# Collecting the sample columns of the feature-major projections in one SBUF tile before they go to DRAM

## The chip, the cores and the metric

The kernel runs on one core of one Trainium2 chip. The metric is the device time of one execution in microseconds (us); the median of three runs is quoted. Instructions run on TensorE (PE, with its weight loads as PEld), VectorE (DVE), ScalarE (ACT), GpSimd (POOL) and SyncE (SP). SP does no arithmetic here: it issues most DMAs, in order, from one queue; ACT issues some from its own.

## The reference

One inference step of a two-layer decoder, for a prompt of 2048 tokens and for a sample group of 8 rows with one token each; both share the weights. In each layer:

```
hn   = rms_norm(x) * norm_w
proj = hn @ w_in[l]                       # 1024 -> 3336 columns, split into 15 pieces
r_q, r_k, r_v, r_g                        # retention, rotary on q and k
m_q, m_k, m_v, m_o, m_g, m_i, m_f         # mLSTM
s_u, s_g                                  # S5, a diagonal complex state space model
a_q, a_g                                  # attention into 256 memory tokens
mix  = [ret | mlstm | s5 | memxattn], each times silu of its gate
y    = x + mix @ w_out[l]
```

A last RMSNorm follows. The sample rows go through the same projection, then start from states and caches that are inputs. All results are float32.

## The kernel before

**Tiling.** The prompt is cut into four units of 512 tokens (b = 0 to 3) per layer (l = 0, 1). A unit runs the groups of `ORDER`, each 256 columns of `w_in` (or of `w_out` for out0 to out3 of the unit before it). Matrices are split into a high and a low float32r part, so a product costs three matmuls per 128 rows of contraction. From b = 1 on the split weights come back from DRAM (`ws`), in 8 loads of 256 KB per group.

**Two layouts.** Groups in `FEAT` (m_k, m_q, a_q, s_g, a_g, s_u, r_q) are computed feature-major by `feat_bank`: PSUM holds 128 features by up to 512 tokens, in two halves m. The others are token-major.

**The sample columns.** The 8 sample rows ride along in unit b = 1 of each layer as columns 512 to 519 of `hT`. There a feature-major half is computed in two pieces of 260 columns, and the last 8 columns of the second piece are the sample's. `group` copies them with VectorE into a small tile of 128 x 8 (`sm`, line 480) and stores that with a DMA into `sproj[l]`, a DRAM tile of 8 rows by 3336 columns. The address pattern is

```python
self.dma(AP(self.sproj[l], COL[g] + 128 * m, [[1, 128], [D_IN, NB]]), o)
```

so each of the 1024 elements goes to a place of its own: neighbours in a partition lie 3336 floats apart, and the partitions lie 4 bytes apart. There are 7 groups x 2 halves x 2 layers = 28 such stores. For token-major groups `sample_group` stores whole rows of 256 columns from a tile of 8 partitions (`sproj<-so`).

**Who reads them.** After group r_g of unit b = 1, `sample_layer` starts as a side generator. It reloads every piece from `sproj` in the layout that it wants (`sq`, `sqs`, `srv`, `smq` and so on). Later `sample_s5` fills `uT`, the s_u columns with features on partitions 96 to 127, with 8 DMAs of 32 x 8 single elements.

**Order.** `build` steps the main generator and then all side generators (S5, mLSTM, retention and attention of the prompt, and the sample's). The instruction order on each engine and each DMA queue is then settled by the tile framework, which runs its own timeline when it schedules; it may move independent instructions past each other. S5 of the prompt (`s_core`) stores U to DRAM (`ud<-U`), reads it back permuted on ACT's queue (`X<-ud`, line 194), and loads tables per quarter on SP's (`sTW`, `sWi`, `sCS`); its matmuls are `ps<-X,sWi` and `ps<-X,sTW`. Its result goes through DRAM too, by eight DMAs `yd<-Y` per unit, in pieces of 128 floats. The mLSTM of the prompt makes `E`, `RT`, `rows` and `sm` (lines 799 to 943).

Line 181 is the matmul helper `mm`, line 185 the transpose helper `tr`, line 188 the ACT helper `act`, lines 191 and 194 the DMA helpers of SP and of ACT.

Of the kernel before, what the change touches and what calls it, by code (L numbers as in the profile page):

```python
# [28 lines left out]
D_IN = 3336  # L29
# [4 lines left out]
NB = 8  # L34
WB = 16
KEPT = (0, 1, 2, 3)
FEAT = ("m_k", "m_q", "a_q", "s_g", "a_g", "s_u", "r_q")

COL = dict(r_q=0, r_k=256, r_v=512, r_g=768, m_q=1024, m_k=1280, m_v=1536, m_o=1792, m_g=2048,
           m_if=2304, s_u=2312, s_g=2568, a_q=2824, a_g=3080)  # L40
# [74 lines left out]
def AP(t, off, ap):  # L115
    return bass.AP(tensor=t.tensor, offset=t.offset + off, ap=[list(x) for x in ap])


class Builder:
# [93 lines left out]
    def setup(self):  # L213
        nc, I, cp = self.nc, self.I, self.cp
        c = lambda n, s, dt=F32: cp.tile(s, dt, name=n, tag=n)
        self.ident = c("ident", [128, 128])
        self.dma(self.ident, I["c_ident"])
        self.wstream()
        self.mem_load()
        self.wload(0)  # L220
        self.hnl = self.hn_load(0, 0)
        next(self.hnl)
        self.wload(1)
        self.maskb = c("maskb", [128, 512], BF16)
        self.identb = c("identb", [128, 128], BF16)
        mt = self.t2([128, 512])
        self.dma(mt, I["c_mask"])
        nc.vector.tensor_copy(self.maskb, mt)
        nc.vector.tensor_copy(self.identb, self.ident)
        self.Dt = c("Dt", [128, 2, 2, 128])  # L230
        self.dma(self.Dt, I["c_D"])
        self.vd = c("vd", [128, H])
        self.dma(self.vd, I["c_vd"])
        self.ropes = c("ropes", [128, 2, 16])
        self.dma(self.ropes, I["c_ropes"])
        self.smc = c("smc", [128, 4])
        self.dma(self.smc, I["c_sm"])
        self.e127 = c("e127", [128, 1])
        self.dma(self.e127, I["c_e127"])
        self.s32 = c("s32", [128, 32])  # L240
        self.dma(self.s32, I["c_s32"])
        self.s8 = c("s8", [128, 8])
        self.dma(self.s8, I["c_s8"])
        st = self.t2([128, H])
        self.dma(st, I["c_sel"])
        self.sel = c("sel", [128, H], F32R)
        nc.vector.tensor_copy(self.sel, st)
        zero = self.t2([128, 320])
        nc.vector.memset(zero, 0.0)
        self.ones = c("ones", [128, 1])  # L250
        nc.vector.memset(self.ones, 1.0)

        self.hT = [cp.tile([128, 8, UT + NB], F32R, name=f"hT{i}", tag=f"hT{i}") for i in range(2)]
        self.Sr = [c(f"Sr{i}", [128, 2, 128]) for i in range(3)]
        self.Cm = [c(f"Cm{i}", [128, 2, 130]) for i in range(3)]
        for t in self.Sr + self.Cm:
            nc.vector.memset(t, 0.0)
        self.mprev = c("mprev", [4, 8])
        self.hS = [c(f"hS{i}", [128, 8, 40], F32R) for i in range(2)]
        for i in range(2):  # L260
            nc.vector.tensor_copy(self.hS[i].rearrange("p a b -> p (a b)"), zero)

        T = self.T
        self.xd = [self.dram([T, D], f"xd{i}") for i in range(self.depth)]
        self.xsd = [self.dram([NB, D], f"xsd{i}") for i in range(self.depth)]
        self.sproj = [self.dram([NB, D_IN], f"sproj{i}") for i in range(self.depth)]
        self.smix = [self.dram([NB, D], f"smix{i}") for i in range(self.depth)]
        self.stab = []
        self.memd = []
        for l in range(self.depth):  # L270
            self.stab.append(dict(
                Wi=self.dram([128, SG, 128], f"Wi{l}"), TW=self.dram([128, 3, 1024], f"TW{l}"),
                CS=self.dram([128, 2, SG, 128], f"CS{l}"), Kd=self.dram([32, 16, 112], f"Kd{l}"), ab=self.dram([128, 3, SG], f"ab{l}"),
                C1=self.dram([128, SG, SC], f"C1{l}")))
            self.memd.append((self.dram([128, 2, MEM], f"mk{l}"), self.dram([128, 2, GW], f"mv{l}")))
# [173 lines left out]
    def group(self, i):  # L449
        kind, l, b, g = self.wseq[i]  # L450
        if i == 0:
            self.wsplit(0, 0)
            self.wsplit(0, 1)
        hi, lo, _ = self.wspl[i]
        if kind == "mem":
            self.mem_group(l, b, hi, lo)
            self.advance(i, 0)
            self.advance(i, 1)
            yield
        elif kind == "out":  # L460
            if self.sample_in_unit(kind, l, b):
                while not self.smix_done[l]:
                    self.step_sides()
                self.sample_group(i, l, g, hi, lo, kind)
            yield from self.group_out(i, l, b, g, hi, lo)
        elif g in FEAT:
            if g == "r_q":
                for m in range(2):
                    self.u["rq", m] = self.g4([128, 2, UT], n="rqt")
                    self.dmaa(self.u["rq", m], self.I["c_rq"][b, m])  # L470
            smp = self.sample_in_unit(kind, l, b)
            pieces = [(0, 260), (260, 520)] if smp else [(0, UT)]
            for m in range(2):
                for c0, c1 in pieces:
                    ps = self.feat_bank(m, hi, lo, slice(c0, c1))
                    c2 = min(c1, UT)
                    self.evac_f(l, b, g, m, ps[:, :c2 - c0], slice(c0, c2))
                    if c1 > UT:
                        o = self.sm([128, 16])[:, :NB]
                        self.nc.vector.tensor_copy(o, ps[:, c2 - c0:c1 - c0])  # L480
                        self.dma(AP(self.sproj[l], COL[g] + 128 * m, [[1, 128], [D_IN, NB]]), o)
                    if (c0, m) == (0, 0):
                        self.advance(i, 0)
                    if c1 >= UT and m == 1:
                        self.advance(i, 1)
                    yield
        else:
            if g == "m_v":
                jobs = [[t] for t in range(4)]
            else:  # L490
                jobs = [[0, 1], [2, 3]]
            n = 264 if g == "m_v" else 256
            for m, ts in enumerate(jobs):
                sls = [slice(t * 128, (t + 1) * 128) for t in ts]
                ps = self.tok_bank(sls, n, hi, lo, self.hslice)
                self.evac(l, b, g, m, ps)
                if m in (0, len(jobs) - 1):
                    self.advance(i, min(m, 1))
                if g == "r_g":
                    nxt = self.next_unit(l, b)  # L500
                    if nxt:
                        self.hn_T(2 * m)
                        self.hn_T(2 * m + 1)
                yield
        if kind == "in" and g not in FEAT and self.sample_in_unit(kind, l, b):
            self.sample_group(i, l, g, hi, lo, kind)
# [1031 lines left out]
    def sample_group(self, i, l, g, hi, lo, kind):  # L1538
# [16 lines left out]
        else:  # L1555
# [5 lines left out]
            if g == 3:  # L1561
# [3 lines left out]
                else:  # L1565
                    w = self.bcrow(self.I["final_norm_w"])
                    self.rms_rows([self.xrow], w[:NB], NB)
                    self.dma(self.O["y_sample"].rearrange("b o d -> (b o) d"), self.xrow)

    def s_load(self, t, l, name, width, off=0, outer=True):  # L1570


        for q in range(4):
            o = COL[name] + (q * 16 if width == 16 else 0)
            self.dma(t[32 * q:32 * q + 32], AP(self.sproj[l], o, [[D_IN, NB], [DH, H], [1, width]]))
# [197 lines left out]
    def sample_s5(self, l, lc):  # L1773
        nc, v, gp, I, O = self.nc, self.nc.vector, self.nc.gpsimd, self.I, self.O
        tab, dr = self.stab[l], self.sproj[l]
# [6 lines left out]

        uT = self.s64([128, 8, NB], n="suT")
        for pr in range(8):
            self.dma(uT[96:128, pr, :], AP(dr, COL["s_u"] + 32 * pr, [[1, 32], [D_IN, NB]]))
        st = self.t1([128, 2, 128], n="sst")
        for w, nme in enumerate(("state_s5_re", "state_s5_im")):
            src = I[nme][l].rearrange("b g p -> (b g) p")
# [3 lines left out]
        ps = self.bank()  # L1792
# [18 lines left out]
        ps = self.bank()  # L1811
# [17 lines left out]
        ps = self.bank()  # L1829
# [15 lines left out]
        g, th = self.t1([128, GW], n="sgg")[:NB], self.t1([128, GW], n="sgh")[:NB]  # L1845
# [144 lines left out]
```

## Time and profile before

| | |
|---|---|
| median of 3 runs | 2325.03 us (2319.82 to 2328.7) |
| the profiled execution, its own time | 2328.93 us |
| its span, first to last instruction | 2327.1 us |
| PE busy | 2160.1 us, 93% |
| DVE, ACT, POOL busy | 61%, 33%, 17% |
| mean granted TensorE clock | 0.962 of full speed |
| DMA packets | 392905, of which 115800 under 512 B |

The span is the time from the first to the last instruction; the execution's own time is 1.8 us more. The mean granted clock is 1 at 2.4 GHz and 0.5 at 1.2 GHz. A matmul record can last longer because the clock is low, so a busy PE is not always a PE at its peak.

### The profile page before, as it was taken

Reading aid. Unit: us, or ns where it says so; the run is one execution under the profiler, and the core shown is the slowest. Engines: PE = TensorE matmul, PEld = TensorE weight load, DVE = VectorE, ACT = ScalarE, POOL = GpSimd, SP = SyncE. Lnnn points to the kernel's source line nnn. Section 1 sums busy time; section 2 is a strip of 40 time slices with the busy share of each in tenths; the row PEclk is TensorE's granted clock in tenths of the full one; section 3 lists DMA queues with packets and bytes.
Section 4 is the critical chain, followed back from the end, with each engine's and each line's share of the span. In section 5 each row is a group of like instructions: output and inputs, shape, how many; then the busy total and the mean of one; then the engine's idle time right before and its main releaser. Section 6 shows DMA issues by size and latency. Waiting matters only on the chain. (4 is left out here: it accounts for less than half of the span.)

```text
span 2327.1 us, 44458 instructions
## 1 busy us (share of the span) xinstructions
PE 2160.1 (93%) x16386; PEld 1991.0 (86%) x16386; DVE 1424.2 (61%) x3883; ACT 778.3 (33%) x1842; POOL 405.5 (17%) x435
## 2 busy tenths in 40 slices
PE   7889977899999999989899999898999899999998
PEld 6688967899997888888798989887899788888888
DVE  7787855535465687565944768355465466656463
ACT  4445422323223332134422454222331233312332
POOL 3343111111001113120202331110100001121011
PEclk9999988999999999989999999898999999999999
DMA  7878587978686656877568884996877776598634
GB/s 223 297 251 270 201 163 140 225 257 139 175 276 202 219 187 214 294 146 230 160 199 281 267 275 149 242 287 132 176 142 258 273 222 209 185 315 211 180 116 153
DMA packets 392905, 496.88 MB, mean 214 GB/s; under 512 B 115800, under 2 KB 216344, under 8 KB 392688
## 3 DMA queue, kind: packets, MB, share of 16 engines
q1 hardware_dynamic: 366848, 433.61, 64.3%
q10 hardware_dynamic: 25840, 60.43, 8.8%
q8 instruction: 129, 2.11, 0.4%
q14 instruction: 88, 0.72, 0.1%
HBM read 376.75 MB, written 118.21 MB: 213 GB/s over the span
## 5 line engine op out<-in xcount | busy, mean ns | idle before, releaser
L181 PE MATMUL pm<-hT,w 128*128 128x512 f32 (+1 forms) x3360 | 681.4, 358 | 9.2 <-ACT w L188 5.9
L181 PEld LDWEIGHTS pm<-hT,w 128*128 128x128 f32 x3360 | 550.7, 193 | 98.1 <-ACT w L188 6.5
L181 PE MATMUL pm<-w,hT 128*128 128x256 f32 (+1 forms) x4608 | 607.8, 288 | 12.8 <-DMA w<-ws 5.0
L181 PEld LDWEIGHTS pm<-w,hT 128*128 128x128 f32 x4608 | 574.1, 193 | 21.4 <-DMA w<-ws 7.2
L181 PE MATMUL pm<-w,mix 128*128 128x256 f32 x3072 | 379.8, 285 | 3.7 <-ACT w L188 2.1
L181 PEld LDWEIGHTS pm<-w,mix 128*128 128x128 f32 x3072 | 372.8, 192 | 4.9 <-ACT w L188 2.3
L366 POOL TENSOR_TENSOR w<-w,w 128x512 fp32r<-128x512 f32 (+1 forms) x76 | 110.0, 1448 | 370.4 <-ACT w L188 158.9
L188 ACT ACTIVATE w<-w 128x512 fp32r<-128x512 f32 (+1 forms) x152 | 95.0, 633 | 181.2 <-DMA w<-w_in 78.1
L1358 POOL TENSOR_TENSOR sA<-sy,sCS 128x512 f32<-128x512 f32 x32 | 53.0, 1658 | 363.1 <-DVE sy L1355 162.0
L366 DVE TENSOR_TENSOR w<-w,w 128x512 fp32r<-128x512 f32 (+1 forms) x76 | 54.6, 720 | 87.7 <-ACT w L188 73.2
L188 ACT ACTIVATE Pt<-ps,sm 128x256 f32<-128x256 f32 x128 | 58.9, 472 | 114.5 <-DVE sm L994 93.0
L1454 DVE TENSOR_TENSOR xr<-xr,pm 128x512 f32<-128x512 f32 x56 | 38.2, 684 | 78.2 <-PE pm L181 32.4
L188 ACT ACTIVATE sB<-ps 64x512 f32<-64x512 f32 x64 | 37.9, 592 | 107.9 <-DVE sy L1347 83.7
L1355 DVE TENSOR_TENSOR_SCAN sy<-ab,xprev,sy 128x128 f32<-128x128 f32 x128 | 57.3, 505 | 0.6
L1414 POOL TENSOR_TENSOR t<-t,s_g 128x512 f32<-128x512 f32 x16 | 25.4, 1584 | 175.2 <-DVE t L1412 83.7
L643 POOL TENSOR_TENSOR r_k<-rp 128x256 f32<-128x256 f32 x32 | 24.2, 759 | 181.8 <-DVE rp L641 160.3
L993 DVE TENSOR_REDUCE sm<-ps 128x2 f32<-128x512 f32 x64 | 42.3, 685 | 21.2 <-PE ps L181 20.9
L181 PE MATMUL ps<-X,sWi 128*128 128x128 f32 x256 | 38.6, 297 | 17.2 <-DMA sWi<-Wi 11.2
L588 POOL TENSOR_TENSOR r_qT<-rqs,rqs 128x512 f32<-128x512 f32 (+2 forms) x20 | 22.0, 1100 | 184.5 <-DVE rqs L587 100.3
L898 POOL TENSOR_TENSOR vw<-mv,RT 128x260 f32<-128x260 f32 x32 | 22.1, 699 | 178.5 <-DVE sm L1109 69.4
L181 PEld LDWEIGHTS ps<-X,sWi 128*128 128x128 f32 x256 | 33.1, 202 | 21.6 <-issue 21.5
L185 PE MATMUL ps<-ident,xt 128*128 128x128 f32 x256 | 38.2, 300 | 13.2 <-DVE xt L387 11.5
(434 smaller groups left out, 3308.5 us busy)
## 6 DMA issues: line engine op xcount, KB each, us to landing
w<-ws SPq DMA_DIRECT2D x768, 256.0 KB
ws<-w SPq DMA_DIRECT2D x256, 256.0 KB
w<-w_in SPq DMA_DIRECT2D x104, 256.0 KB
sCS<-CS SPq DMA_DIRECT2D x32, 512.0 KB
xd<-xr SPq DMA_DIRECT2D x56, 256.0 KB
w<-ws SPq DMA_DIRECT2D x48, 264.0 KB
sTW<-TW SPq DMA_DIRECT2D x32, 384.0 KB
xt<-x_prompt ACTq DMA_DIRECT2D x16, 512.0 KB
```

Of the source, the lines that this page charges most:

```text
L181: self.nc.tensor.matmul(out, lhsT, rhs, start=start, stop=stop, skip_group_check=skip)
L185: self.nc.tensor.transpose(out, in_, self.ident[:K, :K])
L188: self.nc.scalar.activation(out, in_, f, **kw)
L366: e.tensor_tensor(lo[q], r[q], hi[q].bitcast(F32), OP.subtract)
L588: self.nc.gpsimd.tensor_tensor(u["r_qT"][:, m, c], q, qs, OP.add)
L643: gp.tensor_tensor(dst[:, x, :], t1.rearrange("p h f -> p (h f)"), t2.rearrange("p h w f -> p (h w f)"), OP.add)
L898: gp.tensor_tensor(vw, mv[:, j], RT[:, j, 3, :, None].to_broadcast([128, H, 65]), OP.mult)
L993: v.tensor_reduce(mx[:, 2 * x:2 * x + 2], ps[x].rearrange("p (a m) -> p a m", a=2), AX.X, OP.max)
L1355: v.tensor_tensor_scan(t1[:, g], self.abt[:, 2, gg:gg + 1].to_broadcast([128, 128]), t1[:, g], self.xprev[:, gg:gg + 1], OP.mult, OP.add)
L1358: gp.tensor_tensor(A[:, :, 1:129], t1, Cs, OP.mult)
L1414: gp.tensor_tensor(zg.rearrange("p (j s) -> p j s", s=4), z.rearrange("p (s j) -> p j s", s=4), u["s_g", m].rearrange("p (j s) -> p j s", ...
L1454: v.tensor_tensor(xr, xr, ps.rearrange("p (t c) -> p t c", t=2), OP.add)
```

## The change

The sample columns of all 14 feature-major halves of a layer are copied into one tile `sft` of 128 x 14 x 8, one slot per half. When the fourteenth is in, a new side generator `sample_feat` transposes the tile once on TensorE (112 rows of 128), copies the result to SBUF with ACT, and stores it with seven DMAs, one per group, each 16 rows of 128 contiguous floats. `sample_s5` fills `uT` with eight ACT copies out of `sft` in place of eight DMAs from `sproj`.

```diff
                     if c1 > UT:
-                        o = self.sm([128, 16])[:, :NB]
-                        self.nc.vector.tensor_copy(o, ps[:, c2 - c0:c1 - c0])
-                        self.dma(AP(self.sproj[l], COL[g] + 128 * m, [[1, 128], [D_IN, NB]]), o)
+                        if "sft" not in self.u:
+                            self.u["sft"] = self.tb([128, 2 * len(FEAT), NB], "sft")
+                            self.u["sft_n"] = 0
+                        self.nc.vector.tensor_copy(self.u["sft"][:, 2 * FEAT.index(g) + m, :], ps[:, c2 - c0:c1 - c0])
+                        self.u["sft_n"] += 1
+                        if self.u["sft_n"] == 2 * len(FEAT):
+                            self.sides.append(self.sample_feat(l, self.u["sft"]))
...
+    def sample_feat(self, l, sft):
+
+        self.sft[l] = sft
+        yield
+        n = 2 * len(FEAT) * NB
+        ps = self.bank()
+        self.tr(ps[:n, :128], sft.rearrange("p g b -> p (g b)"))
+        o = self.t1([128, 264], n="sfo")
+        self.act(o[:n, :128], ps[:n, :128])
+        for i, g in enumerate(FEAT):
+            self.dma(AP(self.sproj[l], COL[g], [[128, 2], [D_IN, NB], [1, 128]]), o[2 * NB * i:2 * NB * (i + 1), :128])
...
         for pr in range(8):
-            self.dma(uT[96:128, pr, :], AP(dr, COL["s_u"] + 32 * pr, [[1, 32], [D_IN, NB]]))
+            self.act(uT[96:128, pr, :], self.sft[l][32 * (pr % 4):32 * (pr % 4) + 32, 2 * FEAT.index("s_u") + pr // 4, :])
```

## Rows read from the trace of the kernel before

**Rows 1.** The page: span, and busy time, share and instructions of PE.

```profile
span 2327.1 us, 44458 instructions
PE 2160.1 (93%) x16386; PEld 1991.0 (86%) x16386; DVE 1424.2 (61%) x3883; ACT 778.3 (33%) x1842; POOL 405.5 (17%) x435
```

**Rows 2.** Windows by unit: length, busy time of each engine, clock, DMA share, GB/s.

```profile
267.10:607.10 340.00, 298.10 (x2448) 286.27 (x2447) 181.63 (x453) 106.77 (x271) 48.20 (x46) 0.92 0.78 177
607.10:862.90 255.80, 248.90 (x1850) 226.97 (x1849) 159.21 (x519) 79.77 (x190) 26.89 (x36) 0.99 0.70 219
862.90:1141.40 278.50, 267.33 (x1960) 240.04 (x1958) 189.18 (x470) 89.37 (x208) 60.23 (x74) 0.97 0.70 211
1141.40:1422.90 281.50, 267.16 (x1974) 243.93 (x1975) 176.22 (x437) 108.73 (x245) 58.98 (x54) 0.97 0.74 239
1422.90:1730.60 307.70, 276.79 (x2310) 267.93 (x2308) 164.31 (x445) 97.89 (x247) 39.63 (x41) 0.93 0.82 192
1730.60:1984.40 253.80, 247.06 (x1846) 225.48 (x1845) 146.52 (x442) 74.80 (x185) 21.09 (x23) 0.99 0.71 234
1984.40:2257.20 272.80, 264.12 (x1939) 237.98 (x1938) 168.61 (x430) 77.08 (x197) 43.30 (x34) 0.98 0.68 202
```

**Rows 3.** Tile sproj: the DMAs, ns min/median/max to issue, first and last start.

```profile
L191 SPq DMA_DIRECT2D sproj<-sm x28: 367/385/1882, 306.7 to 1713.8; - x28
...
L191 SPq DMA_DIRECT2D suT<-sproj x16: 302/432/884, 940.5 to 2069.6; - x16
```

**Rows 4.** Windows before and after the first store, and while yd is stored.

```profile
295.00:306.00 11.00, 11.00 (x101) 10.43 (x100) 10.55 (x33) 4.03 (x11) 5.27 (x5) 1.00 0.86 289
309.00:314.00 5.00, 5.00 (x44) 5.00 (x44) 3.20 (x12) 1.29 (x4) 0.00 (x0) 1.00 1.00 81
1871.00:1875.00 4.00, 4.00 (x19) 3.26 (x18) 3.23 (x13) 0.08 (x1) 0.00 (x0) 1.00 1.00 338
```

**Rows 5.** DMA rate in 40 slices of 1 us, from 360 us on.

```profile
GB/s 16 45 137 279 379 294 320 54 25 23 10 48 31 71 66 180 250 397 385 412 373 262 303 147 8 3 36 32 41 47 41 269 179 0 16 0 0 0 0 0
```

**Rows 6.** Timeline of SP: a store in that stretch; four stores of yd.

```profile
361.63 0.43 SPq L191 DMA_DIRECT2D sproj<-sm  x1
...
1871.11 1.83 SPq L191 DMA_DIRECT2D yd<-Y  x4
```

**Rows 7.** Timeline of SP, ACT, DVE and PE, 320 to 335 us.

```profile
321.85 0.82 SPq L191 DMA_DIRECT2D sproj<-sm  x1
...
330.60 2.63 ACTq L194 DMA_DIRECT2D X<-ud  x4
333.28 0.66 ACT L188 ACTIVATE mkT<-pm 128x260 f32<-128x260 f32 x2 [11.14 <-issue]
333.97 0.17 DVE L480 COPY sm<-pm 128x8 f32<-128x8 f32 x1 [11.18 <-ACT mkT L188]
334.36 0.58 PE L181 MATMUL ps<-sm,e 128*128 128x16 f32 x2 [7.38 <-DVE sm L862]
```

**Rows 8.** Windows, PE alone, low-clock stretches of each b = 1 unit, with sums.

```profile
332.20:349.30 17.10, 8.98 (x40) 0.50 0.80 124
...
sum 54.80, PE 36.59; mean PE 5.23
...
sum 41.00, PE 27.90; mean PE 5.58
```

**Rows 9.** Tile and group views: what the new transpose and copies are like.

```profile
L185 PE MATMUL ps<-ident,mkT x64: 270/272/421, 104.0 to 2090.5; 128*128 128x128 f32 x64
...
L188 ACT ACTIVATE sso<-ps 128x128 f32<-128x128 f32 x2 | 0.6, 278 | 17.9 <-PE ps L185 14.9 <-issue 3.0
```

**Rows 10.** Timeline of SP: the first sample load of layer 1.

```profile
1729.15 0.76 SPq L191 DMA_DIRECT2D sq<-sproj  x1
```

**Rows 11.** Waits of SP's queue.

```profile
SPq L191 <- PE pm L181: 325.6, 233, 18.6
...
SPq L191 <- DVE sm L480: 15.9, 6, 8.7
```

More of the change, by code (lines that the diff above doesn't have):

```diff
@@ L268, in setup @@
         self.stab = []
+        self.sft = {}
         self.memd = []
```

## Prediction

> **What bounds the kernel now.** I read the page first. PE is busy for 2160.1 of 2327.1 us, so time comes back only where PE stands still or runs at its low clock [rows 1]. The next view is the windows, cut where each unit's last r_g bank is evacuated. The reader should compare the two b = 1 units, rows one and five of the table, with the other five [rows 2]. They last 340.0 and 307.7 us; the others 253.8 to 281.5. They are the units that carry the sample columns. They have more PE work, but PE is also idle in them for 340.00 - 298.10 = 41.9 and 307.70 - 276.79 = 30.9 us, against 6.9, 11.2, 14.3, 6.7 and 8.7 in the others, on average 9.6. The granted clock is 0.92 and 0.93 against 0.97 to 0.99. And their DMA engines are the busier ones for less work: shares of 0.78 and 0.82 at 177 and 192 GB/s, where the others have 0.68 to 0.74 at 202 to 239.
>
> The view of the tile sproj shows what is special there: 28 stores `sproj<-sm`, the first at 306.7 us, the last at 1713.8 [rows 3]. SP needs 0.385 us to issue one, so the issue is cheap. The windows around the first one show the price. Before it the DMA engines move 289 GB/s at a share of 0.86; from 309 to 314 us they move 81 GB/s at a share of 1.00 [rows 4]. They are full and deliver little. In slices of 1 us from 360 us on the rate is 279 to 379 GB/s in the four slices from 363 to 367, then eight slices in a row stay under 75, and from 384 seven more do [rows 5]. The first of these runs follows the store issued at 361.63 us, once the packets ahead of it are through [rows 6]. So one store of 4 KB blocks the engines for some 8 us, and everything in their queues waits with it.
>
> How that reaches PE is seen in the timeline from 320 to 335 us [rows 7]. The store of 321.85 us goes out while ACT wants to issue `X<-ud`; it reads back what `ud<-U` has stored, and starts only at 330.60. ACT's queue is in order, so the evacuation of mkT waits behind it, 11.14 us in all. The copy at line 480 reads the same bank and waits 11.18 us on VectorE's queue, and a small PE matmul behind that finds PE idle for 7.38 us. After such a gap the clock falls to the lower of the two levels, 0.50 from 332.2 to 349.3 us; summed over such stretches PE is busy at half clock for 36.59 us in the first of the units and for 27.90 us in the second [rows 8].
>
> **The change, part by part.** *Removed: 28 scattered stores.* All of the excess is an upper bound. Idle time is 41.9 + 30.9 = 72.8 us [rows 2]. Work done at half clock takes twice as long, so half of 36.59 + 27.90, or 32.2 us, is lost to the clock [rows 8]. Together 105.0 us. Not all of it will go, since units without these stores have idle time too. I let the two units sink to the level of the other five: 9.6 us idle each, and a clock loss that I scale. There the mean clock misses 2% of 268.5 us, or 5.4 us [rows 2]; in the b = 1 units the loss of 32.2 us stands against a missing 0.08 x 340.0 + 0.07 x 307.7 = 48.7 us of clock, a share of 0.66, as part of the low clock falls on idle time. So 0.66 x 5.4 = 3.6 us stay. What stays is 2 x (9.6 + 3.6) = 26.4 us, and the gain is 105.0 - 26.4 = 78.6 us. The lower bound is that only the waits nearest to the stores go and other waits appear behind them. I put it at half of that, 39 us. I take 78.6 because the mechanism repeats at each store and because nothing else sets these units apart from their neighbours.
>
> A second working gives the same order. The b = 1 units moved about 340.0 x 177 = 60 MB and 307.7 x 192 = 59 MB; their neighbours 255.8 x 219 = 56 and 253.8 x 234 = 59 MB [rows 2]. The load on the queues is not larger, so without the blocks these loads can flow as in a neighbour.
>
> *Replaced: where the copy goes.* The 28 copies stay as they are, 128 x 8, 0.17 us [rows 7]. No gain and no loss.
>
> *Added: transpose, copy, seven stores per layer.* One transpose of 128 x 112 takes about 0.27 us, as the row of mkT has it, so 0.5 us of PE in all [rows 9]. One ACT copy of 112 x 128 takes about 0.28 us, as `sso` does [rows 9]; ACT is busy for 106.77 and 97.89 us of these units and has room [rows 2]. Seven issues replace fourteen on SP, at about 0.385 us each [rows 3], so SP gains 2.7 us per layer, which hides behind its other waits. The stores write 16 pieces of 512 B each. How such pieces fare is visible in `yd<-Y`: four DMAs are issued from 1871.1 us on, and the engines move 338 GB/s at a share of 1.00 [rows 4, 6]; these are pieces of 512 B too, by their address pattern. So I take the seven at nothing on the engines; the bound is one old store's block, 8 us of engine time per layer, spread over PE as before: 78.6 / 28 = 2.8 us each, 5.6 us for two.
>
> *Moved: when the rows reach DRAM.* All feature-major groups now arrive after the last half of a_g. In layer 1 the last store goes out at 1713.8 us [rows 3], and the first reload `sq<-sproj` is issued at 1729.15 us [rows 10]. That leaves 15.4 us for a transpose, a copy and 7 x 0.385 = 2.7 us of issues. If the cover were gone, SP would hold at `sq` with the weight loads behind it, for at most the missing time.
>
> *Removed: 16 loads of uT; added: 16 ACT copies.* SP loses eight issues of 0.43 us per layer [rows 3]. A copy of 32 x 8 is bounded by 0.28 us, so ACT gets 2.2 us per layer [rows 9], in units where it is busy for 77 to 89 of 270 us [rows 2]. The loads read single elements and start at 940.5 us [rows 3], in units with the ordinary idle time; I count no gain.
>
> Sum: 2328.93 - 78.6 + 0.5 = 2250.8 us for an execution like the profiled one. That execution lies 3.9 us above the median of the runs, so for the median 2246.9, or 2247 us.
>
> **The rivals.** *Half of it (the partial case).* The stalls go, but the waits move to other loads of the same queues, because PE's order is dense and ACT and SP still hold at every DMA that waits. The gain is 39 us, the time 2286. For it: the SP queue waits 325.6 us for PE in any case [rows 11], and the units' order was made with these stores in it. Against it: neighbours with as many bytes show 9.6 us of idle time.
>
> *The stores were never the cost.* If a 4-byte piece costs only its own slot, 1024 pieces are 64 on each of 16 engines, and the low rate has another source, such as the `yd` and `ud` traffic of S5, which stays. Then PE's gaps stay, and with the added 0.5 us the time is 2325.5 us. For it: 4 KB is next to nothing beside the 60 MB of a unit. Against it: yd's own stores leave the rate at 338 GB/s, with no such fall as from 309 to 314 us [rows 4], and the other five units have the same S5 traffic without the idle time.
>
> The Trainium skill, page "DMA: Bandwidth & Descriptors", section "Why small descriptors are slow (HBM only)", gives a fixed overhead of some 3 bus cycles per piece and 32 B of metadata; with the 850 MHz that it names for the fabric, my estimate from it is 64 x 4 cycles, 0.3 us per store. By that rule the removed stores were worth 28 x 0.3 = 8 us of hidden DMA time, this rival holds and the time would be about 2325; the 5 us at a share of 1.00 and 81 GB/s differ from it, and I go by the row.
>
> *Slower.* The seven stores stand in SP's in-order queue and wait for the ACT copy, which waits for the transpose, which waits in PE's order for the last copy of a_g. Weight loads behind them wait too. The old stores did this for VectorE's copy six times, 8.7 us at the longest; SP's longest wait of all is 18.6 us [rows 11]. To eat the gain and 12 us more, the hold would have to cost PE (78.6 + 12) / 2 = 45 us per layer. At the longest wait shown, twice 18.6, the result is 2247 + 37 = 2284, still faster; beyond 45 us per hold, some 2337.
>
> *More than all.* Loads run ahead so well that nothing of the excess stays: 105 us and some knock-on, 2215.
>
> **How the numbers follow.** What a measurement can tell from no change is about 0.5%, 11.6 us. I draw the line between the forecast and the partial case midway, at a gain of 59 us. Chances: my forecast, 59 to 105 us, 0.66; the partial case, 12 to 59 us, 0.22; no change 0.06; slower 0.03; more than all 0.03. So faster has 0.91, no change 0.06, slower 0.03. The range runs from 2218 (the upper bound, 105 us, and 2 more) to 2288 (just past the partial case). What it leaves out is the last three cases, 0.12, and some 0.06 of the partial one.
>
> **What the new profile would show.** Right: no `sproj<-sm`; 14 stores of rows, after a_g; b = 1 units of about 340.0 - 47 = 293 and 307.7 - 32 = 276 us, with idle time near 10 us and a clock of 0.97 or more; no run of slices under 75 GB/s at a full share. The unit figures are the excess of each: 41.9 + 18.3 - 13.2 = 47 less what the new work takes, and 30.9 + 14.0 - 13.2 = 32. Wrong: low rates at full share remain, then the stores were not the cause; or the rate is high and PE still waits, then the order or the queues hold it. A long SP wait ahead of the seven stores would be the slower case.

## The result, and the profile after

The changed kernel takes 2223.44 us, median of 4 runs (2219.64 to 2227.03), against 2326.75 us for the kernel before, beside it: a ratio of 0.956 with an interval of 0.953 to 0.959. That is 103 us less. The forecast was 2247 us within 2218 to 2288. The direction was right; the gain was 78.6 us on paper and is larger by 25.

The page of the changed kernel: PE does the same work in a shorter span, and the small packets are fewer by 33000, the 28672 elements of the stores and the 4096 of the uT loads among them.

```profile
span 2223.7 us, 44414 instructions
...
PE 2128.1 (96%) x16388; PEld 1965.0 (88%) x16388; DVE 1426.7 (64%) x3883; ACT 782.1 (35%) x1860; POOL 404.9 (18%) x435
...
DMA packets 359685, 496.86 MB, mean 223 GB/s; under 512 B 82356, under 2 KB 183124, under 8 KB 359468
```

The windows by unit of the changed kernel, columns as in [rows 2]. The first and the fifth are the b = 1 units.

```profile
265.90:554.70 288.80, 282.79 (x2449) 273.33 (x2448) 181.41 (x455) 107.60 (x271) 47.16 (x46) 0.99 0.65 209
554.70:813.20 258.50, 249.38 (x1849) 227.10 (x1848) 158.98 (x519) 79.81 (x189) 27.01 (x36) 0.98 0.68 217
813.20:1083.80 270.60, 264.34 (x1960) 237.79 (x1958) 189.70 (x469) 91.14 (x216) 60.37 (x75) 0.99 0.71 217
1083.80:1367.10 283.30, 268.60 (x1974) 245.43 (x1975) 177.42 (x438) 108.80 (x246) 59.08 (x53) 0.96 0.73 237
1367.10:1629.80 262.70, 262.70 (x2309) 256.37 (x2308) 165.09 (x444) 97.68 (x247) 39.95 (x41) 1.00 0.66 226
1629.80:1884.40 254.60, 248.23 (x1847) 226.66 (x1845) 146.58 (x442) 74.80 (x184) 21.08 (x23) 0.99 0.71 232
1884.40:2154.40 270.00, 262.04 (x1939) 236.22 (x1938) 171.08 (x430) 78.61 (x205) 43.34 (x34) 0.99 0.69 205
```

Beside [rows 2]: the b = 1 units fall from 340.0 to 288.8 and from 307.7 to 262.7 us, together by 96.2 of the 103.4 us of span. Their idle time falls from 41.9 to 6.0 and from 30.9 to 0.0 us, their clock rises to 0.99 and 1.00, and the DMA engines are less busy (0.65 and 0.66) while they move more in the same time (209 and 226 GB/s). Of the other five, the two b = 3 units (third and last row) are shorter by 7.9 and 2.8 us; the rest are longer, by up to 2.7 us.

The low-clock stretches of the first of these units, PE alone, answer to [rows 8]: 6.8 us in place of 54.8. In the second there are none.

```profile
326.70:330.10 3.40, 3.40 (x16) 0.50 0.64 191
391.50:394.90 3.40, 3.40 (x17) 0.50 1.05 366
```

The DMA rate in 40 slices of 1 us from 300 us on, while s_u and m_k are computed, answers to [rows 5]: one slice alone is under 98 GB/s.

```profile
GB/s 266 326 365 406 310 109 217 285 242 269 310 307 213 207 215 307 387 397 369 365 261 214 182 235 261 282 98 109 164 340 82 301 252 301 289 387 402 402 385 154
```

What the new work costs, from the views of the tiles sft and sfo (ns min/median/max, first and last start):

```profile
L483 DVE COPY sft<-pm x28: 134/160/168, 305.0 to 1611.0; 128x8 f32<-128x8 f32 x28
L188 ACT ACTIVATE suT<-sft x16: 204/206/208, 886.9 to 1949.4; 32x8 f32<-32x8 f32 x16
...
L185 PE MATMUL ps<-ident,sft x2: 270/270/270, 537.3 to 1612.8; 128*112 128x128 f32 x2
...
L191 SPq DMA_DIRECT2D sproj<-sfo x14: 567/567/707, 537.9 to 1617.2; - x14
L188 ACT ACTIVATE sfo<-ps x2: 277/278/279, 537.6 to 1613.1; 112x128 f32<-112x128 f32 x2
```

SP's timeline from the stores of rows to the first reload, in layer 0 and then in layer 1:

```profile
537.88 4.46 SPq L191 DMA_DIRECT2D sproj<-sfo  x7
...
554.20 0.75 SPq L191 DMA_DIRECT2D sq<-sproj  x1
```

```profile
1613.37 4.44 SPq L191 DMA_DIRECT2D sproj<-sfo  x7
1617.91 3.73 SPq L191 DMA_DIRECT2D w<-ws  x8
1621.74 0.49 SPq L191 DMA_DIRECT2D sproj<-so  x1
1622.28 0.72 SPq L191 DMA_DIRECT2D sq<-sproj  x1
```

The DMA engines while the seven stores of layer 0 go out, and right after, in windows with the columns of [rows 4]:

```profile
539.00:543.00 4.00, 4.00 (x36) 3.96 (x36) 3.99 (x5) 0.98 (x2) 0.00 (x0) 1.00 0.05 14
544.00:546.00 2.00, 2.00 (x20) 2.00 (x19) 0.00 (x0) 0.00 (x0) 0.00 (x0) 1.00 0.97 314
```

And the waits of SP's queue, as in [rows 11]:

```profile
SPq L191 <- ACT sfo L188: 16.1, 2, 9.7
```

The transpose and the copy cost what [rows 9] said. An issue of the row stores takes 0.567 us, not 0.385, and the seven take 4.46 us with the gaps between them. They leave the engines at a share of 0.05. SP does hold for the ACT copy, up to 9.7 us, in layer 1. PE pays nothing for it: the unit in which that hold lies has no idle time at all.

### The profile page after: what moved, and what is told of

It reads as the page before. It is cut to its first block, busy times and chain, and to the rows that moved or that the text cites. A ratio compares the mean times of both kernels' runs of the same rounds, so it can differ in the third digit from the quotient of the medians.

```text
span 2223.7 us, 44414 instructions
## 1 busy us (share of the span) xinstructions
PE 2128.1 (96%) x16388; PEld 1965.0 (88%) x16388; DVE 1426.7 (64%) x3883; ACT 782.1 (35%) x1860; POOL 404.9 (18%) x435
## 4 chain that ended last, share of the span: by engine, by line
PE 48%; DMA 4%; DVE 3%; issue 2%; ACT 1%; SPq 0%; POOL 0%; ACTq 0%; DVEq 0%; POOLq 0%
PE pm L181 36%; PE ps L181 9%; PE ps L185 2%; DMA w<-ws 1%; DMA xd<-xr 1%; SPq L191 0%; DMA xr<-xd 0%; DMA xr<-x_prompt 0%; DMA fx<-xd 0%; DMA sK<-cache_mem_v 0%; DVE xt L388 0%; DMA smx<-smix 0%; DMA CS<-snt 0%; ACT Pt L188 0%; DVE sm L208 0%
## 5 line engine op out<-in xcount | busy, mean ns | idle before, releaser
L181 PEld LDWEIGHTS pm<-hT,w 128*128 128x128 f32 x3360 | 544.7, 190 | 99.4 <-ACT w L188 6.6
L181 PE MATMUL pm<-w,hT 128*128 128x256 f32 (+1 forms) x4608 | 599.0, 286 | 9.6 <-DVE w L367 3.9
L181 PEld LDWEIGHTS pm<-w,hT 128*128 128x128 f32 x4608 | 566.5, 190 | 16.9 <-ACT hT L188 4.9
L1363 POOL TENSOR_TENSOR sA<-sy,sCS 128x512 f32<-128x512 f32 x32 | 53.6, 1676 | 355.4 <-DVE sy L1360 210.8
L185 PE MATMUL ps<-ident,xt 128*128 128x128 f32 x256 | 37.3, 294 | 13.7 <-DVE xt L388 11.4
L207 DVE TENSOR_TENSOR sm<-sm 128x8 f32<-128x8 f32 (+4 forms) x210 | 45.8, 219 | 4.7
L1352 DVE TENSOR_TENSOR sy<-ps,sCS 128x512 f32<-128x512 f32 x32 | 22.1, 690 | 40.1 <-PE ps L181 34.7
```

What stands on the lines that cost most here:

```text
L181: self.nc.tensor.matmul(out, lhsT, rhs, start=start, stop=stop, skip_group_check=skip)
L185: self.nc.tensor.transpose(out, in_, self.ident[:K, :K])
L207: v.tensor_tensor(t, y, y, OP.mult)
L1363: gp.tensor_tensor(A[:, :, 1:129], t1, Cs, OP.mult)
```

## The experiments

Four theories stood at the start. **A**: each scattered store into DRAM blocks the DMA engines, and PE pays for it. **B**: single-element transfers cost by their number, loads and stores alike. **C and D**: not the store but the waiting on it, or the instruction order that the scheduler finds. All medians below are set against the kernel before by a ratio measured on the same chip; the differences in us between experiments are of medians, in part from different chips. The changed kernel itself came out at 2223.44 and, measured again, at 2225.18 us.

**Undo the uT part.**

```diff
-            self.act(uT[96:128, pr, :], self.sft[l][...])
+            self.dma(uT[96:128, pr, :], AP(dr, COL["s_u"] + 32 * pr, [[1, 32], [D_IN, NB]]))
```

> The change with one part undone: uT is again filled by 16 DMAs of 256 single elements from the DRAM rows. Theory A (the 28 scattered stores into DRAM were the whole cost): the median stays at that of the changed kernel, 2223 us, within 6 us. Rival B (single-element transfers cost by their number, loads and stores alike): the 4096 elements of the loads are one eighth of all 32768, so 13 us of the 103 come back, about 2236 us.

Measured: 2234.98 us, ratio 0.961 (0.959 to 0.963). The number is that of rival B, 11.5 us above the changed kernel. The b = 1 units last 287.5 and 263.9 us, as in the changed kernel, so the stores of rows alone bring back nearly all of the gain. What differs lies in the b = 3 units, where uT is filled; it is taken up further down.

**Undo the store part.** The tile is filled and uT comes from it, but the old stores stay.

```diff
+                        self.dma(AP(self.sproj[l], COL[g] + 128 * m, [[1, 128], [D_IN, NB]]), self.u["sft"][...])
...
-        self.tr(ps[:n, :128], sft.rearrange("p g b -> p (g b)"))
...
-            self.dma(AP(self.sproj[l], COL[g], [[128, 2], [D_IN, NB], [1, 128]]), o[...])
```

> The other half: the tile sft is filled and uT is read from it, but each half is also stored from it at once by the old scattered store, and there is no transpose and no store of rows. Theory A: back to the kernel before, 2326 us, within 10 us, and both b = 1 units above 300 us. Rival B: one eighth of the gain stays, about 2313 us. Rival D (the instruction order that the scheduler finds is what changed): any time between 2223 and 2326, with the DMA rate low after each store all the same.

Measured: 2330.9 us, ratio 1.004 (1.002 to 1.007). As theory A had it, with both b = 1 units long:

```profile
264.10:605.70 341.60, 295.07 (x2448) 283.72 (x2447) 181.24 (x455) 107.42 (x270) 47.56 (x46) 0.92 0.79 175
862.30:1135.50 273.20, 266.00 (x1960) 239.15 (x1958) 186.72 (x468) 91.26 (x217) 59.42 (x75) 0.98 0.72 214
1414.20:1736.40 322.20, 279.97 (x2309) 270.71 (x2308) 166.03 (x444) 97.37 (x247) 40.04 (x41) 0.92 0.84 184
1989.20:2261.10 271.90, 261.88 (x1940) 236.01 (x1940) 171.31 (x430) 78.77 (x206) 42.69 (x34) 0.99 0.69 203
```

These are the b = 1 and b = 3 units. The b = 3 units are 5.3 and 0.9 us shorter than in [rows 2], but the b = 1 units are 16 us longer in all, and the sum shows no gain. Rival B's eighth did not stay.

**Add the stores back, read by nobody; then half of them.**

```diff
+        self.scr = [self.dram([NB, D_IN], f"scr{i}") for i in range(self.depth)]
...
+                        self.dma(AP(self.scr[l], COL[g] + 128 * m, [[1, 128], [D_IN, NB]]), self.u["sft"][...])
```

The second kernel has `if m == 0:` ahead of the store.

> The changed kernel with the 28 scattered stores added back, into a scratch DRAM tile of the same pitch that nobody reads; the results still come by the rows. Theory A (the store itself blocks the DMA engines for some 8 us): the gain of 103 us is gone, 2315 to 2340 us. Rival C (the cost was the waiting of later transfers on these stores, through the shared DRAM tile): little comes back, 2223 to 2250 us.

> The same with half of the stores, those of m = 0, 14 in all. Theory A with an equal price for each store (103 / 28 = 3.7 us): 2223 + 51 = 2275 us, within 15 us. Rival: only stores that fall close together cost, as their blocks add up; then well under half comes back, 2223 to 2250 us.

Measured: 2329.47 us with 28 (ratio 1.001, 0.999 to 1.003) and 2273.23 us with 14 (0.977, 0.974 to 0.980). The whole gain goes with the stores, and half of it with half of them: 106 / 28 = 3.8 and 50 / 14 = 3.6 us each. Nobody reads the scratch tile, so the shared DRAM tile and the waits on it (rival C) were not needed for the loss. The rival that only crowded stores hurt fell too. The b = 1 units, first of the kernel with 28, then of the one with 14:

```profile
263.10:610.50 347.40, 295.82 (x2449) 283.92 (x2448) 182.16 (x455) 107.60 (x272) 47.43 (x46) 0.92 0.77 174
1426.60:1743.10 316.50, 278.77 (x2310) 268.83 (x2309) 165.33 (x445) 97.67 (x248) 40.56 (x41) 0.93 0.81 188
```

```profile
266.20:578.20 312.00, 288.99 (x2448) 278.51 (x2447) 182.44 (x455) 107.48 (x271) 47.87 (x46) 0.96 0.74 193
1385.40:1673.20 287.80, 272.27 (x2310) 264.15 (x2309) 165.86 (x444) 97.56 (x248) 40.07 (x41) 0.96 0.78 207
```

With 28 stores they have the clock and the DMA rate of the kernel before, and more idle time, 51.6 and 37.7 us; with 14 they lie between. As in the kernel with the uT part alone, the two units are 16 us longer in all than in the kernel before, so the equal total contains the gain of the uT part (below). Why stores out of `sft` cost these units more than those out of `sm` was not tested. The order of the instructions differs in all of these kernels, so order (rival D) does not explain a loss that follows the count.

**What in the store costs?** Five kernels add 28 DMAs in the same place, of 4 KB each, and change the pieces, the target or the direction. First, single elements into a dense block:

```diff
+        self.scr = [self.dram([14, NB, 128], f"scr{i}") for i in range(self.depth)]
...
+                        self.dma(self.scr[l][2 * FEAT.index(g) + m].rearrange("b p -> p b"), self.u["sft"][...])
```

> The changed kernel with 28 scattered stores added, single elements again, but each store goes into a dense block of 4 KB (neighbours of a partition lie 512 B apart, the partitions 4 B apart) that nobody reads. Theory A1 (what costs is the single-element write to DRAM, wherever it lands): the gain is gone, 2310 to 2340 us. Rival A2 (the pitch of 13344 B is what hurts): 2223 to 2245 us.

Measured: 2328.35 us, ratio 1.003 (1.000 to 1.005). The pitch is not the cause. The first store is issued at 302.56 us. The DMA rate in slices of 0.5 us from 300 us on:

```profile
GB/s 393 397 422 353 179 162 225 180 209 377 334 103 48 21 18 18 43 23 49 43 39 47 20 10 12 29 20 14 23 143 363 328 328 397 352 377 393 397 406 406
```

The seventeen slices from 306 to 314.5 us, 8.5 us in all, stay under 50 GB/s. The windows of such a stretch, first of the kernel before, then of this one, and SP's issue of the six weight loads behind the store, first here, then with the pieces of 32 B that follow:

```profile
310.00:317.50 7.50, 7.50 (x65) 7.50 (x64) 3.68 (x14) 3.61 (x9) 0.00 (x0) 1.00 0.88 37
306.00:314.50 8.50, 8.50 (x73) 8.50 (x72) 2.57 (x10) 2.50 (x6) 0.00 (x0) 1.00 0.65 28
```

```profile
306.09 9.44 SPq L191 DMA_DIRECT2D w<-ws  x6
309.09 2.75 SPq L191 DMA_DIRECT2D w<-ws  x6
```

The engines are busy for 0.88 and 0.65 of the stretch, and SP needs 9.44 us for issues that take 2.75 us behind a store in 32 B pieces. So the store holds up the queue behind it.

Then pieces of 32 B, and later of 8 B:

```diff
+                        self.dma(self.scr[l][2 * FEAT.index(g) + m], self.u["sft"][...])   # scr: [14, 128, NB]
...
+                        self.dma(self.scr[l][2 * FEAT.index(g) + m, :, :, 0:2], ...)       # scr: [14, 128, 4, 4]
```

> The same 28 stores of 4 KB, but in 128 pieces of 32 B, eight times fewer. If each piece costs the same (103 us for 28672 pieces): 3584 pieces give 13 us, 2236 us. If each store of small pieces costs the same, whatever their number: 2310 us and more. If it goes by bytes, also 2310 us and more.

> The changed kernel with 28 stores of 4 KB added in pieces of two floats (8 B), 512 pieces each, into a scratch DRAM tile. If every piece under some size costs the same: half of the 4-byte case, 2223 + 51 = 2275 us. If a store costs by its bytes as long as the pieces are that small: 2310 us and more. If only single floats hurt: 2223 to 2235 us, as with 32 B pieces.

Measured: 2227.92 us with 32 B (0.959, 0.957 to 0.961) and 2245.69 us with 8 B (0.965, 0.963 to 0.968; the changed kernel on that chip 2225.18). With 32 B the medians leave 4.5 us for all 28, which the intervals do not tell from nothing; with 8 B it is 20.5 us, or 0.7 each. The price of a store does not go by its bytes, which are the same, nor in proportion to its pieces: 1024, 512 and 128 pieces give 3.7, 0.7 and 0.2 us, the last not told from nothing. None of the three laws in the 8 B expectation fits. The rate in slices of 0.5 us from 300 us on, first with 32 B, where stores are issued at 305.56 and 314.50 us, then with 8 B, where one is at 305.37:

```profile
GB/s 258 279 287 332 352 393 406 393 365 209 121 189 211 168 193 373 328 148 225 267 268 268 307 328 217 262 336 356 402 397 279 311 414 381 339 376 198 205 291 308
```

```profile
GB/s 246 209 250 311 377 410 402 402 375 215 115 258 205 180 274 401 194 75 4 10 78 104 201 207 231 270 275 252 270 315 402 406 414 385 369 393 414 366 321 296
```

In these 20 us there is no fall under 120 GB/s with 32 B; with 8 B four slices, 2 us, stay under 80.

Then single elements, but into SBUF, and single elements loaded from DRAM:

```diff
+                        self.dma(self.sm([128, 16]).rearrange("p (b x) -> p b x", x=2)[:, :, 0], self.u["sft"][...])
...
+                        self.dma(self.sm([128, 16])[:, :NB], AP(self.I["w_in"][l], COL[g] + 128 * m, [[1, 128], [D_IN, NB]]))
```

> The same 28 stores of 1024 single elements, but into a tile in SBUF, every second float. Theory A (the write to DRAM is what blocks the engines): 2223 to 2240 us, and no run of low DMA rate after them. Rival E (the engines are slow with any single-element piece): 2310 us and more.

> In place of added stores, 28 loads of 1024 single elements each from a DRAM weight with the same pitch, into a small SBUF tile that nobody reads. If loads cost as stores do: 2310 us and more. If the 11.5 us that came back with the 4096 elements of the uT loads are a price of each element: 28672 / 4096 x 11.5 = 80 us, 2304 us. If those 11.5 us came by another way (order, SP's queue) and loads are cheap: 2223 to 2245 us.

Measured: 2229.36 us into SBUF (0.959, 0.957 to 0.962) and 2225.36 us for the loads (0.958, 0.953 to 0.964). Neither costs anything that can be told from nothing. The rate with the stores into SBUF, issued at 304.61 and 313.05 us, in the same slices, does not fall under 139 GB/s; with the loads, issued at 306.34, 311.38 and 319.30 us, not under 108:

```profile
GB/s 274 340 279 373 402 410 381 303 184 139 230 164 274 303 357 168 211 231 307 309 317 283 229 279 250 332 332 307 320 352 385 377 373 293 278 300 348 279 307 186
```

```profile
GB/s 182 285 256 277 295 262 283 233 275 352 344 385 385 402 404 323 112 108 259 156 147 328 401 176 137 231 277 178 131 279 188 299 352 295 295 315 332 295 352 418
```

So neither the number of packets nor the cutting into elements is enough by itself: the loss takes small writes into DRAM. What it is about them was not separated. At 4 KB per store the size and the number of the pieces change together. And wherever 4 B pieces went into DRAM, the partitions lay 4 B apart, so pieces of eight partitions share each 32 B of DRAM; in the kernels with 8 B and 32 B every partition had a stretch of its own. A store of 4-byte pieces that do not lie side by side was not run.

**The 11.5 us of the uT loads.** Three kernels on one chip: the changed one, the one with the uT loads restored, and the changed one with the loads added into a tile that nobody reads.

```diff
+            self.dma(uD[96:128, pr, :], AP(dr, COL["s_u"] + 32 * pr, [[1, 32], [D_IN, NB]]))
```

> The changed kernel once more, beside the next two on one chip, to tell whether the 11.5 us that the uT loads brought back hold: 2223 us, within 5 us.

> The kernel with the uT loads restored, once more. If the 11.5 us are of this kernel: 8 to 15 us above the changed kernel of the same chip. If they were the difference of two chips: within 4 us of it.

> The changed kernel, uT by ACT copies, with the 16 single-element loads added back into a tile that nobody reads. If the loads themselves cost (their transfers or their places in SP's queue): as much as the kernel with the uT loads restored, about 2235 us. If it is the wait of the S5 sample work for them, or the order that goes with it: the time of the changed kernel, 2223 us, within 4 us.

Measured: 2225.18 us (0.958, 0.955 to 0.960), 2237.35 us (0.962, 0.959 to 0.965) and 2236.71 us (0.962, 0.959 to 0.964). The 12 us hold and come with the loads even when nobody waits for their data. The b = 3 units of the changed kernel on this chip, then of the one with the idle loads:

```profile
808.60:1078.20 269.60, 264.12 (x1960) 237.81 (x1958) 188.67 (x470) 91.53 (x216) 60.22 (x74) 0.99 0.72 217
1878.50:2149.40 270.90, 261.33 (x1939) 235.20 (x1938) 170.68 (x430) 78.83 (x206) 43.16 (x34) 0.99 0.69 204
```

```profile
814.40:1088.30 273.90, 265.58 (x1960) 239.11 (x1958) 189.41 (x468) 91.35 (x217) 60.06 (x75) 0.98 0.73 214
1887.20:2169.50 282.30, 267.47 (x1939) 238.39 (x1939) 172.47 (x430) 78.88 (x206) 42.67 (x34) 0.97 0.68 196
```

They are 4.3 and 11.4 us longer, with more idle time (8.3 and 14.8 us against 5.5 and 9.6) and a lower clock. A price of each element is excluded by the loads in the b = 1 units, seven times as many for 2 us, where it asked for 80. What is left is the place of eight DMAs in SP's queue at that point, or the order that the scheduler makes around them. The traces point to the queue. In layer 1 SP spends most of the time from 1956.70 to 1963.44 us on issuing seven of these loads, and at the end of it the engines stand nearly empty, at a share of 0.23 and 17 GB/s. PE's waits for weight loads in that unit are 9.1 us, against 2.9 in the changed kernel (total, times, longest):

```profile
1961.50:1963.50 2.00, 2.00 (x19) 2.00 (x18) 2.00 (x3) 0.00 (x0) 0.00 (x0) 1.00 0.23 17
```

```profile
PE pm L181 <- DMA w<-ws: 9.1, 7, 3.1
PE pm L181 <- DMA w<-ws: 2.9, 4, 1.5
```

But no run held the order fixed, so it stays open.

## Why the prediction was right, and where it was too small

*The cause.* "One store of 4 KB blocks the engines for some 8 us, and everything in their queues waits with it": shown, by adding the stores back without a reader, by half of them, and by the slices after them. "Full" was too strong: the window of [rows 4] begins ahead of the fall, and over the low stretch the share is 0.88, or 0.65 with the dense block. Without the stores the two units keep none of their excess of idle time, so nothing else of weight sets them apart.

*Removed: 28 scattered stores.* The term was mis-sized. Of 72.8 us idle, 66.8 went, not 53.6; of 32.2 us lost to the clock, 32.2 - 6.8 / 2 = 28.8 went, not 25.0. Together that is 95.6 in place of 78.6 us. The step that failed is that the two units would sink to the level of their neighbours, 9.6 us idle and 3.6 us of clock each. They sank below it, to 6.0 and 0.0 us idle, and last 288.8 and 262.7 us where 293 and 276 were forecast: the neighbours' remaining waits are not a floor for every unit. The uT loads in two of the five (below) explain little of this, as the five still idle 8.9 us on average in the changed kernel. Why the b = 1 units can do with less was not tested. Over the whole kernel the term is somewhat smaller than in the two units: with the uT loads kept, the rows alone gain 2323.64 - 2234.98 = 88.7 us on their chip.

*Replaced and added.* Copy, transpose and ACT copy as priced. The row stores take 0.567 us to issue in place of 0.385, and 4.5 us for seven; hidden. Taking their engine time at nothing was right: the engines are at a share of 0.05 while the seven go out and at 314 GB/s right after, and even 32 B pieces cost nothing that can be told.

*Moved.* In layer 1, for which the forecast worked out the cover, the last row store has been issued at 1613.37 + 4.44 = 1617.8 us, and the first reload goes out at 1622.28. Of the 15.4 us only 4.5 are left; it was enough, as SP has weight loads to issue in between and shows no hold. In layer 0 the cover is 11.9 us, from 537.88 + 4.46 = 542.3 to 554.20.

*Removed: uT loads.* "I count no gain" was wrong: 12 us of the whole, by two kernels on one chip. With the 88.7 us of the rows that makes up the 103, within the noise. So of the 25 us that the forecast lacked about 10 are the stores' and 12 the uT loads'. The parts need not add in every order: while the old stores stayed, the uT part brought nothing.

*The rivals.* The partial case did not come. "The stores were never the cost" fell: a store takes 8 us of the engines. The rule that the Trainium skill gives, page "DMA: Bandwidth & Descriptors", section "Why small descriptors are slow (HBM only)", a few bus cycles per piece, is not contradicted by the loads and the stores into SBUF, which cost nothing that can be told here; for 4-byte writes to DRAM this case's runs differ from it by more than a factor of 20 (8.5 against the estimated 0.3 us). The slower rival's mechanism exists, as SP held 9.7 us for the ACT copy, but it cost PE nothing that can be seen, far from the 45 us per layer that this rival needed. The result lies in the forecast's own case, 59 to 105 us, at its upper end, and "more than all" did not come.

## What to carry to other kernels

When DMA engines are busy (a share of 0.65 to 0.88 here) and move a tenth of their rate, look for the DMA issued some microseconds earlier with the smallest pieces on its DRAM side: its own issue may be cheap (0.39 us) while the queues behind it pay, and PE shows it mostly as waits on other work, such as an evacuation behind an ACT queue that can't issue, and as a low clock. Turn such a store round on chip, or make its pieces 32 B long, with a stretch of its own for each partition, and keep single elements for loads or for SBUF. A unit's excess over its neighbours is a fair estimate of what such a cause costs, but not an upper bound on the gain: work out the bound of all idle and low-clock time too. Here the gain in the two units, 95.6 us, lay between the two, 78.6 and 105.

## What the runs showed of the hardware that was not expected

A store of 1024 single floats into DRAM holds the rate of all DMA engines under 75 GB/s for some 8 us, dense or scattered; the same 4 KB in 8 B pieces for 2 us, in 32 B pieces not at all in the stretch shown. The same elements into SBUF, or loaded from DRAM, leave the rate as it was. The Trainium skill, page "DMA: Bandwidth & Descriptors", section Specifications, draws the line at 512 B, with a read-modify-write below; here 32 B pieces cost nothing that can be told, and a cost shows with 8 B and 4 B, and only for writes into DRAM. Whether a read-modify-write is behind it, and whether the size, the number or the neighbourhood of the pieces decides, no run here shows.
